# Feature-major products of a fp32 decoder block: the low halves of the weights stored at shifted addresses

## The chip, the cores and the metric

The kernel runs on one core of a Trainium2 chip. The metric is device time of one execution in microseconds: the median of several executions. A profile is taken of one further execution; its span is the time from the first to the last recorded instruction.

The engines are named as in the profile: PE is TensorE (matrix products), PEld its loading of weights, DVE is VectorE, ACT is ScalarE, POOL is GpSimd, SP is SyncE, which here issues the loads of weights from memory.

## The reference

One layer of a decoder trunk on 256 positions of 2048 features in fp32. Cut to what is computed:

```
h = rms_norm(x, norm_mix_pre);  proj = h @ w_in
a_in, b_in, q, kv, nsa_g, merge_g = split(proj)
y_a = conformer_conv(a_in, ...)            # GLU, depthwise conv of 31, LayerNorm, swish, @ w_a_out
y_b = chunked_spatial_gating(b_in, ...)    # gelu, LayerNorm, 128x128 mixing, @ w_b_out
y_c = native_sparse_attention(q, kv, ...)  # compressed, selected and window branches, @ w_c_out
mixed = (g_a * y_a + g_b * y_b + g_c * y_c) @ w_o
x = x + rms_norm(mixed, norm_mix_post)
h = rms_norm(x, norm_ffn_pre)
u = causal_depthwise_conv(h @ w_up);  u_g, u_v = split(u)
x = x + rms_norm((silu(u_g) * u_v) @ w_down, norm_ffn_post)
```

Nearly all of the arithmetic is in the products with `w_in`, `w_up` and `w_down`.

## The kernel before

**Numbers in two parts.** TensorE multiplies in a rounded form of fp32 (float32r, `R` in the code). To keep precision, each operand is split: a head `hi` (the value copied to float32r by ScalarE) and a rest `lo` (the value minus its head, by VectorE). A product is the sum of head x head, head x rest and rest x head.

**Weights.** Each block of weights, 128 partitions x 1024 columns (512 KB), comes by one DMA on SP's queue into one of five `wraw` buffers (`fetch`, line 100). `piece` (line 128) then makes the head with one ScalarE copy (line 143) into one of four `whi` buffers, and the rest with one VectorE subtraction (line 144) into one of four `wlo` buffers. `raw.name` numbers them: `whi72` and `wlo72` belong to `wraw72`. `split2` (line 108) does the same in two halves for the first product of the program.

**Feature-major products.** `ftile` (line 150) computes 128 output features for all 256 positions. Its weights are the stationary operand and come as two pieces (`granule`): k-tiles 0 to 7 and 8 to 15, each k-tile 128 columns, so 512 bytes of a partition's row. The activations are the moving operand: `hT` (first layer) or `h2T` (second layer), laid out as k-tile, part (head, rest), position. `lumps` (line 161) writes the matmuls of one tile in three groups:

- `h(0..7)`: weight heads x both parts of the activation, 512 moving columns (line 172);
- `l(0..15)`: weight rests x the head of the activation, 256 moving columns (line 179);
- `h(8..15)`: as the first, for the last eight k-tiles.

Each matmul has weights of its own, so each has a weight load. The load for the next matmul runs while the present one streams its moving columns. There are 40 such tiles with `hT` (conformer input, gating input, keys and values, queries) and 88 with `h2T` (`w_up`). Of those 88, the first two are written out by hand around the end of the first layer (`up_hi`, `up_lo`, line 1064, with the loop at line 1028 and the `fixed` order at 1078 to 1100), and the third at lines 1125 to 1156. The other products (merge gates, `w_o`, `w_down` and so on) have activations as the stationary operand and weights as the moving one (`mm_t`, `mm`); their weights pass through the same `whi` and `wlo` buffers.

**What sets the order.** Each engine runs its instructions in the order of the built program. The Tile framework sets it from the order of the code, from priorities (`tc.high_priority`) and from explicit chains (`tc.issue_after`). Background work stands in generators (`conv_gen` for the 31-tap convolution, line 475, `sg_gen`, `attn`), from which `pump` takes some after each tile. In the first layer VectorE does the rests, the sums of finished tiles (`fsum`, lines 215 and 217) and that convolution.

**Other names.** `rb2` (line 1118) holds the second layer's scale per position, which `fsum` multiplies in for each of the 88 tiles; `junk` (line 303) is a buffer of 1 KB per partition into which ScalarE writes squares of which only the sum is used.

Of the kernel before, what the change touches and what calls it, by code (L numbers as in the profile page):

```python
# [23 lines left out]
F32 = mybir.dt.float32  # L24
R = mybir.dt.float32r
# [6 lines left out]
T = 256  # L32
KT = 16
# [21 lines left out]
def block(ctx: ExitStack, tc: tile.TileContext, x, xf, fp, cst, rows, sgw, w1, w2, wf_a, wt_bv, wf_bu, wf_c,  # L55
          wt_vs, wf_q, wt_g, wt_p, wt_o, wf_up, wt_dn, wt_dq, out):
    nc = tc.nc
    V, S, PE, G = nc.vector, nc.scalar, nc.tensor, nc.gpsimd

    PZ = ctx.enter_context(tc.tile_pool(name="pz", bufs=1))  # L60
    P0 = ctx.enter_context(tc.tile_pool(name="p0", bufs=1))
# [35 lines left out]
    uid = [0]  # L97
# [7 lines left out]

    fetched = [None]

    def split2(raw):

        hi = P0.tile([128, 1024], R, tag="whi", bufs=4, name="s" + raw.name)  # L110
        lo = P0.tile([128, 1024], R, tag="wlo", bufs=4, name="r" + raw.name)
        for c in (slice(0, 512), slice(512, 1024)):
            with chained():
                a = S.activation(hi[:, c], raw[:, c], AF.Copy)
                v = V.tensor_sub(lo[:, c], raw[:, c], hi[:, c].bitcast(F32))
            chain[:] = [a.ins, v.ins]
        return hi, lo
# [7 lines left out]
            order.enter_context(tc.issue_after(ins))  # L125
        return order

    def piece(src, n, into=None):

        raw = fetch(src, n)  # L130
        if into:
            hl = into.pop(0)
            hi, lo = hl[:, 0], hl[:, 1]
        else:
            hi = P0.tile([128, 1024], R, tag="whi", bufs=4, name=f"whi{uid[0]}")
            lo = P0.tile([128, 1024], R, tag="wlo", bufs=4, name=f"wlo{uid[0]}")
        with ExitStack() as order:
            if behind:
                for ins in behind.pop(0):
                    order.enter_context(tc.issue_after(ins))  # L140
            else:
                order.enter_context(tc.high_priority(offset=int(PR)))
            S.activation(hi[:, :n], raw[:, :n], AF.Copy)  # L143
            V.tensor_sub(lo[:, :n], raw[:, :n], hi[:, :n].bitcast(F32))  # L144
        return hi, lo

    def granule(src):
        return [piece(src[:, a:a + 1024], 1024) for a in (0, 1024)]

    def ftile(src, mov):  # L150

        hs = granule(src)
        ps = PS.tile([128, 2, T], F32, tag="acc", name=f"ps{uid[0]}")
        mm_f(ps, hs, mov)
        return ps
# [5 lines left out]
    def lumps(ps, ws, mov, t=None):  # L161

        ts = slice(0, T) if t is None else slice(t * 128, t * 128 + 128)
        n = 8 * len(ws)
        m = 8 if n > 8 else 7

        def h(ks):
            for k in ks:  # L170
                c = (k % 8) * 128
                ins = PE.matmul(ps[:, :, ts], lhsT=ws[k // 8][0][:, c:c + 128], rhs=mov[:, k, :, ts],  # L172
                                start=(k == 0 and not t), stop=(k == n - 1), skip_group_check=t is not None).ins
            return ins

        def l(ks):
            for k in ks:
                c = (k % 8) * 128
                ins = PE.matmul(ps[:, 1, ts], lhsT=ws[k // 8][1][:, c:c + 128], rhs=mov[:, k, 0, ts], start=False,  # L179
                                stop=False, skip_group_check=True).ins  # L180
            return ins
        return [lambda: h(range(m)), lambda: l(range(n)), lambda: h(range(m, n))]
# [791 lines left out]
    def fixed(eng, op, *args, **kw):  # L974

        with ExitStack() as order:
            order.enter_context(tc.high_priority())
            for ins in seq.get(eng, ()):
                order.enter_context(tc.issue_after(ins))
            seq[eng] = [op(*args, **kw).ins]  # L980
# [45 lines left out]
    for n, (cb, p) in enumerate(HELD):  # L1026
        for i in range(2):
            if n == 0 and i == 0:
                pe_last[0] = mm_o(cb, 1, p, held[n], (i,))
            else:  # L1030
                in_line(mm_o, cb, 1, p, held[n], (i,))
            if (n, i) == (3, 1):
                h2 = P0.tile([128, KT, 2, T], R, tag="hT", name="h2T")
            k = 2 * n + i - 7
            if k == 14:
                order_of(order2)
                fixed(S, S.activation, junk, po[3, 1], AF.Square, accum_out=ss1[1][:, 3:4])
            for k in ([k] if 0 <= k < 14 else [14, 15] if k == 14 else []):
                in_line(enter2, 0, k)
                if k % 4 == 3:  # L1040
                    up = wf_up[k // 8][:, k // 4 % 2 * 1024:k // 4 % 2 * 1024 + 1024]
                    if k < 15:
                        behind.append(tuple(order2))
                        ws2[k // 8].append(piece(up, 1024))
                    else:
                        raw = fetch(up, 1024)
        if p == 7 and cb == 2:
            done_o(cb, 1)
# [12 lines left out]

    def up_lo(f, ks):
        for k in ks:
            ins = PE.matmul(pu2[f][:, 1], lhsT=ws2[f][k // 8][1][:, k % 8 * 128:k % 8 * 128 + 128],
                            rhs=h2[:, k, 0], start=False, stop=False, skip_group_check=True).ins
        return ins

# [7 lines left out]
    fixed(V, V.reduce_sum, v1, ss1[1], axis=AX.X)  # L1075
    fixed(V, V.tensor_scalar, v1, v1, 1.0 / D, EPS, op0=ALU.mult, op1=ALU.add)
    fixed(S, S.activation, r1, v1, AF.Sqrt)
    hi, lo = (P0.tile([128, 1024], R, tag=tag, bufs=4, name=tag + "last") for tag in ("whi", "wlo"))
    fixed(S, S.activation, hi, raw, AF.Copy)
    ws2[1].append((hi, lo))  # L1080
    fixed(V, V.reciprocal, r1, r1)
# [6 lines left out]
    for c in range(4):  # L1088
        if c == 0:
            residual(0)  # L1090
            residual(1)
        for k in quarter[c]:
            in_line(enter2, 1, k)
        if c == 0:
            residual(2)
            fixed(V, V.tensor_mul, y1[:, 1, 1536:], po[3, 1], rw[:, 1536:])
            in_line(up_hi, 1, range(12, KT), 0)
        elif c == 1:
            residual(3)
            fixed(V, V.tensor_sub, lo, raw, hi.bitcast(F32))  # L1100
        if c:
            for f in range(2):
                in_line(up_hi, f, quarter[c - 1], 1)
        for f in range(2):
            in_line(up_lo, f, quarter[c])
# [9 lines left out]
    gl = [P2.tile([128, 11, T], R, tag="gl", bufs=4, name=f"gl{i}") for i in range(4)]  # L1115
    P2b = P2b_ctx.enter_context(tc.tile_pool(name="p2b", bufs=1))
    T1["pool"], T1["bufs"] = P2b, 2
    rb2 = P2b.tile([128, T], F32, name="rb2")

    def small(name, shape=(128, T), dt=F32):  # L1120
        return P2b.tile(list(shape), dt, tag="fa", bufs=5, name=name)

    ones2 = small("ones2", (128, 128))
    G.memset(ones2, 1.0)
    raw = [fetch(wf_up[2][:, a:a + 1024], 1024) for a in (0, 1024)]
    hs = []
    for i in range(2):
        hi, lo = (P0.tile([128, 1024], R, tag=tag, bufs=4, name=f"{tag}f2{i}") for tag in ("whi", "wlo"))
        fixed(S, S.activation, hi, raw[i], AF.Copy)
        fixed(V, V.tensor_sub, lo, raw[i], hi.bitcast(F32))  # L1130
        hs.append((hi, lo))
    with ExitStack() as order:
        order.enter_context(tc.high_priority())
# [109 lines left out]
        return hi, lo  # L1243

    def ring(name):
        return [P0.tile([128, 1024], R, tag=tag, bufs=4, name=f"{tag}{name}") for tag in ("whi", "wlo")]

    class Pair:
        def __init__(self, p):
# [265 lines left out]
```

## Time and profile before

| | us |
|---|---|
| median of 3 executions | 1577.27 |
| lowest, highest | 1576.33, 1577.35 |
| the profiled execution | 1577.51 |
| its span | 1575.8 |

A row of the instruction groups reads: line, engine, operation, output<-inputs, shape, count | busy time in us, mean of one in ns | idle time of the engine just before them in us, and what ended it. A timeline row reads: start and length in us, engine, line, operation, and how many like it follow each other. The length of a merged row runs to the end of its last instruction, and a matmul's own length overlaps the next one's start. In the table by stretches, each engine has its busy time and, in brackets, its instructions.

### The profile page before, as it was taken

Reading aid. Unit: us, or ns where it says so; the run is one execution under the profiler, and the core shown is the slowest. Engines: PE = TensorE matmul, PEld = TensorE weight load, DVE = VectorE, ACT = ScalarE, POOL = GpSimd, SP = SyncE. Lnnn points to the kernel's source line nnn. Section 1 sums busy time; section 2 is a strip of 40 time slices with the busy share of each in tenths; the row PEclk is TensorE's granted clock in tenths of the full one; section 3 lists DMA queues with packets and bytes.
Section 4 is the critical chain, followed back from the end, with each engine's and each line's share of the span. In section 5 each row is a group of like instructions: output and inputs, shape, how many; then the busy total and the mean of one; then the engine's idle time right before and its main releaser. Section 6 shows DMA issues by size and latency. Waiting matters only on the chain.

```text
span 1575.8 us, 22359 instructions
## 1 busy us (share of the span) xinstructions
PE 1564.6 (99%) x8178; PEld 1328.5 (84%) x8178; DVE 1232.3 (78%) x2114; ACT 891.8 (57%) x1442; POOL 19.5 (1%) x50
## 2 busy tenths in 40 slices
PE   9999999999999999999999999999999999999997
PEld 7888889888888787788888888888888888888885
DVE  7899999858866555465557988888777777988997
ACT  7644544447646675644456666565555555555563
POOL 1000020000000000000000000000000000000000
PEclk9999999999999999999999999999999999999999
DMA  9555556665764445556774666666566666666674
GB/s 375 177 196 182 189 176 212 193 197 179 235 200 157 159 137 173 160 187 187 243 250 149 204 191 189 191 189 188 187 188 191 191 191 190 200 203 211 207 235 159
DMA packets 85439, 307.94 MB, mean 195 GB/s; under 512 B 9808, under 2 KB 10832, under 8 KB 84304
## 3 DMA queue, kind: packets, MB, share of 16 engines
q1 hardware_dynamic: 83376, 297.84, 59.2%
q0 software_dynamic: 1520, 8.39, 1.5%
q8 instruction: 64, 1.05, 0.3%
q10 hardware_dynamic: 432, 0.28, 0.1%
q14 instruction: 47, 0.39, 0.1%
HBM read 301.23 MB, written 4.19 MB: 194 GB/s over the span
## 4 chain that ended last, share of the span: by engine, by line
PE 96%; DVE 2%; DMA 1%; issue 0%; ACT 0%; DVEq 0%; POOL 0%; ACTq 0%; POOLq 0%
PE ps L172 29%; PE ps L179 15%; PE pg L193 6%; PE pg L192 6%; PE pg L194 6%; PE pd0b L1264 5%; PE pd1a L1264 4%; PE py L193 3%; PE py L194 3%; PE py L192 3%; PE po L192 2%; PE po L194 2%; PE po L193 2%; PE pd0a L1264 2%; PE pd1b L1264 1%; PE pv L192 1%
## 5 line engine op out<-in xcount | busy, mean ns | idle before, releaser
L144 DVE TENSOR_TENSOR wlo<-wraw,whi 128x1024 fp32r<-128x1024 f32 x440 | 535.9, 1221 | 173.6 <-ACT whi L143 167.0
L143 ACT ACTIVATE whi<-wraw 128x1024 fp32r<-128x1024 f32 x440 | 461.4, 1054 | 244.3 <-PE pg L194 98.0
L172 PE MATMUL ps<-h2T,whi 128*128 128x512 f32 x1360 | 325.0, 391 | 0.0
L172 PEld LDWEIGHTS ps<-h2T,whi 128*128 128x128 f32 x1360 | 249.8, 188 | 48.2
L179 PEld LDWEIGHTS ps<-h2T,wlo 128*128 128x128 f32 x1360 | 174.5, 191 | 6.7
L179 PE MATMUL ps<-h2T,wlo 128*128 128x256 f32 x1360 | 176.6, 283 | 0.0
L172 PE MATMUL ps<-hT,whi 128*128 128x512 f32 x640 | 157.5, 392 | 0.0
L214 ACT ACTIVATE t<-ps 128x256 f32<-128x256 f32 x125 | 47.6, 382 | 185.7 <-PE ps L172 185.3
L194 PE MATMUL pg<-whi,hT 128*128 128x512 f32 x384 | 150.9, 393 | 0.0
L193 PE MATMUL pg<-wlo,hT 128*128 128x512 f32 x384 | 150.7, 392 | 0.0
L192 PE MATMUL pg<-whi,hT 128*128 128x512 f32 x384 | 147.8, 393 | 0.0
L172 PEld LDWEIGHTS ps<-hT,whi 128*128 128x128 f32 x640 | 116.2, 189 | 21.3
L215 DVE TENSOR_TENSOR t<-ps,t 128x256 f32<-128x256 f32 x125 | 52.9, 424 | 68.9 <-ACT t L214 68.2
L475 DVE SCALAR_TENSOR_TENSOR cv<-hb,fps,cv 128x256 f32<-128x256 f32 x240 | 105.7, 484 | 0.8 <-ACT cv L471 0.7
L179 PEld LDWEIGHTS ps<-hT,wlo 128*128 128x128 f32 x640 | 84.8, 190 | 4.6
L179 PE MATMUL ps<-hT,wlo 128*128 128x256 f32 x640 | 87.0, 283 | 0.0
L193 PEld LDWEIGHTS pg<-wlo,hT 128*128 128x128 f32 x384 | 72.1, 188 | 16.2 <-issue 1.1
L194 PEld LDWEIGHTS pg<-whi,hT 128*128 128x128 f32 x384 | 72.1, 188 | 15.1 <-issue 0.7
L192 PEld LDWEIGHTS pg<-whi,hT 128*128 128x128 f32 x384 | 71.8, 188 | 14.7 <-issue 0.3
L980 DVE TENSOR_TENSOR wlowraw<-wraw,whiwraw 128x1024 fp32r<-128x1024 f32 x44 | 53.2, 1223 | 11.8 <-ACT whiwraw L980 10.6
L980 ACT ACTIVATE whiwraw<-wraw 128x1024 fp32r<-128x1024 f32 x44 | 45.7, 1054 | 18.1 <-PE pd0b L1264 14.9
L1194 ACT ACTIVATE fa<-fs,fps 128x256 f32<-128x256 f32 x88 | 52.5, 596 | 1.2 <-DVE fs L217 0.9
(1020 smaller groups left out, 2468.1 us busy)
## 6 DMA issues: line engine op xcount, KB each, us to landing
wraw<-in_wf_up_dram SPq DMA_DIRECT2D x176, 512.0 KB, 4.3
wraw<-in_wt_g_dram SPq DMA_DIRECT2D x96, 512.0 KB, 4.3
wraw<-in_wt_p_dram SPq DMA_DIRECT2D x48, 512.0 KB, 4.2
wraw<-in_wt_dn_dram SPq DMA_DIRECT2D x48, 512.0 KB, 4.4
wraw<-in_wt_dq_dram SPq DMA_DIRECT2D x40, 512.0 KB, 4.7
wraw<-in_wf_a_dram SPq DMA_DIRECT2D x32, 512.0 KB, 4.5
wraw<-in_wt_o_dram SPq DMA_DIRECT2D x32, 512.0 KB, 4.5
wraw<-in_wf_bu_dram SPq DMA_DIRECT2D x16, 512.0 KB, 4.5
```

The costliest lines, as they stand in the source:

```text
L143: S.activation(hi[:, :n], raw[:, :n], AF.Copy)
L144: V.tensor_sub(lo[:, :n], raw[:, :n], hi[:, :n].bitcast(F32))
L172: ins = PE.matmul(ps[:, :, ts], lhsT=ws[k // 8][0][:, c:c + 128], rhs=mov[:, k, :, ts], start=(k == 0 and not t), stop=(k == n - 1), skip_ ...
L179: ins = PE.matmul(ps[:, 1, ts], lhsT=ws[k // 8][1][:, c:c + 128], rhs=mov[:, k, 0, ts], start=False, stop=False, skip_group_check=True).ins
L192: PE.matmul(ps, lhsT=xh, rhs=hi, start=first, stop=False)
L193: PE.matmul(ps, lhsT=xh, rhs=lo, start=False, stop=False)
L194: return PE.matmul(ps, lhsT=xl, rhs=hi, start=False, stop=last).ins
L215: V.tensor_add(t1 if rb is not None else dst, ps[:, 0], t1)
L475: V.scalar_tensor_tensor(ca[:, j], hb[:, j, k:k + T], w(j, k), ca[:, j], op0=ALU.mult, op1=ALU.add)
L980: seq[eng] = [op(*args, **kw).ins]
L1194: S.activation(a, s, AF.Identity, bias=fps[:, C_FB + f:C_FB + f + 1], scale=w[2])
L1264: ins = PE.matmul(bank, lhsT=a[x], rhs=w[y], start=first and j == 0, stop=last and j == 2).ins
```

## The change

Rests of feature-major products get rows of 1152 columns instead of 1024 (`rests`), of which each piece uses 1024 and some left free. `spread(k)` gives the place of k-tile `k` in its row: k-tile 0 at column 0 as before, k-tiles 1 to 14 at 16 columns (64 bytes) past their old place, k-tile 15 at 24 columns (96 bytes) past it. All buffers start at a multiple of 512 bytes, before and after. `apart` writes them: the subtraction of one piece becomes two, k-tile 0 and k-tiles 1 to 7 for the first piece (`first` true), k-tiles 8 to 14 and k-tile 15 for the second. The matmuls read the rests at `spread(k)`; heads, activations and all other products stay where they were. Where rests of other products pass through the same buffers, the first 1024 columns are used as before. The four longer buffers take 2 KB of a partition's memory; `rb2` gives back 1 KB by lying in `junk`.

```diff
+    def rests(name):
+        return P0.tile([128, 1152], R, tag="wlo", bufs=4, name=name)
+
+    def spread(k):
+        return k % 8 * 128 + (0, 16, 24)[(k > 0) + (k == KT - 1)]
...
-            V.tensor_sub(lo[:, :n], raw[:, :n], hi[:, :n].bitcast(F32))
+            if first is None:
+                V.tensor_sub(lo[:, :n], raw[:, :n], hi[:, :n].bitcast(F32))
+            else:
+                apart(lo, raw, hi, first)
...
+    def apart(lo, raw, hi, first, do=None):
+
+        for a, b, to in ((0, 128, 0), (128, 1024, 144)) if first else ((0, 896, 16), (896, 1024, 920)):
+            x = (lo[:, to:to + b - a], raw[:, a:b], hi[:, a:b].bitcast(F32))
+            if do:
+                do(V, V.tensor_sub, *x)
+            else:
+                V.tensor_sub(*x)
+
+    def granule(src, feat=False):
+        return [piece(src[:, a:a + 1024], 1024, first=not a if feat else None) for a in (0, 1024)]
...
-        hs = granule(src)
+        hs = granule(src, True)
...
             for k in ks:
-                c = (k % 8) * 128
+                c = spread(k)
                 ins = PE.matmul(ps[:, 1, ts], lhsT=ws[k // 8][1][:, c:c + 128], rhs=mov[:, k, 0, ts], start=False,
...
-            ins = PE.matmul(pu2[f][:, 1], lhsT=ws2[f][k // 8][1][:, k % 8 * 128:k % 8 * 128 + 128],
+            ins = PE.matmul(pu2[f][:, 1], lhsT=ws2[f][k // 8][1][:, spread(k):spread(k) + 128],
...
-    rb2 = P2b.tile([128, T], F32, name="rb2")
...
+    rb2 = junk.bitcast(F32)
```

In the hand-written part the pieces of the first three `w_up` tiles are split by `apart` in the same way (`fixed` gives them their place in VectorE's order). Line numbers grow by 6 to 18 from the first added lines on: line 144 of before is 151 and 163 in the changed kernel (163 for the split rests), 215 is 233, 217 is 235, 475 is 493.

The order on VectorE, in the second layer. `fa` and `fs` are the tiles of the short convolution after `w_up`, `t1` holds half a tile's sum. Before:

```order
L1196 SCALAR_TENSOR_TENSOR fa27_9452<-fs27_9447,fps_65,fa27_9452 128x254
L144 TENSOR_TENSOR wlo351_9584<-wraw351_9581,whi351_9583 128x1024
L1199 TENSOR_TENSOR fa26_9398<-fa26_9398,fa27_9452 128x256
L1170 TENSOR_TENSOR st6_9572<-fa26_9398 128x128
L1203 TENSOR_TENSOR gl1_7886<-fa26_9398,gh1_7882 128x128
L215 TENSOR_TENSOR t1_348_9506<-ps348_9472,t1_348_9506 128x256
L217 SCALAR_TENSOR_TENSOR fs28_9505<-t1_348_9506,rb2_7892 128x256
L144 TENSOR_TENSOR wlo352_9590<-wraw352_9587,whi352_9589 128x1024
```

After the change:

```order
L163 TENSOR_TENSOR wlo351_9723<-wraw351_9720,whi351_9722 128x128
L163 TENSOR_TENSOR wlo351_9723<-wraw351_9720,whi351_9722 128x896
L1214 SCALAR_TENSOR_TENSOR fa27_9587<-fs27_9582,fps_65,fa27_9587 128x254
L1217 TENSOR_TENSOR fa26_9531<-fa26_9531,fa27_9587 128x256
L1188 TENSOR_TENSOR st6_9711<-fa26_9531 128x128
L233 TENSOR_TENSOR t1_348_9643<-ps348_9609,t1_348_9643 128x256
L235 SCALAR_TENSOR_TENSOR fs28_9642<-t1_348_9643,junk_113 128x256
L163 TENSOR_TENSOR wlo352_9730<-wraw352_9727,whi352_9729 128x896
L163 TENSOR_TENSOR wlo352_9730<-wraw352_9727,whi352_9729 128x128
```

Each rest has become two instructions at the same place; two or three small instructions have changed places with them.

The order on VectorE in the first layer, around the last feature tile of the keys and values (`wlo79` and `wlo80`), where VectorE also works on the gating product (`ub`, `Bt`) and the convolution (`cv`). Before:

```order
L144 TENSOR_TENSOR wlo79_2357<-wraw79_2354,whi79_2356 128x1024
L550 TENSOR_TENSOR ub_1451<-ub_1451,sgf6_2153 128x256
L475 SCALAR_TENSOR_TENSOR cv_118<-hb_116,fps_65,cv_118 128x256 x2
L144 TENSOR_TENSOR wlo80_2363<-wraw80_2360,whi80_2362 128x1024
L475 SCALAR_TENSOR_TENSOR cv_118<-hb_116,fps_65,cv_118 128x256
L550 TENSOR_TENSOR ub_1451<-ub_1451,sgf7_2161 128x256
L475 SCALAR_TENSOR_TENSOR cv_118<-hb_116,fps_65,cv_118 128x256 x2
L217 SCALAR_TENSOR_TENSOR kkv_2187<-t1_74_2233,hb_116 128x256
L215 TENSOR_TENSOR t1_76_2288<-ps76_2255,t1_76_2288 128x256
```

After the change:

```order
L163 TENSOR_TENSOR wlo79_2419<-wraw79_2416,whi79_2418 128x896
L568 TENSOR_TENSOR ub_1483<-ub_1483,sgf4_2142 128x256
L568 TENSOR_TENSOR ub_1483<-ub_1483,sgf5_2150 128x256
L235 SCALAR_TENSOR_TENSOR kcv_1953<-t1_72_2202,hb_116 128x256
L568 TENSOR_TENSOR ub_1483<-ub_1483,sgf6_2209 128x256
L493 SCALAR_TENSOR_TENSOR cv_118<-hb_116,fps_65,cv_118 128x256 x2
L568 TENSOR_TENSOR ub_1483<-ub_1483,sgf7_2217 128x256
L233 TENSOR_TENSOR t1_76_2348<-ps76_2315,t1_76_2348 128x256
L235 SCALAR_TENSOR_TENSOR kkv_2243<-t1_74_2291,hb_116 128x256
L493 SCALAR_TENSOR_TENSOR cv_118<-hb_116,fps_65,cv_118 128x256
L163 TENSOR_TENSOR wlo80_2426<-wraw80_2423,whi80_2425 128x896
L163 TENSOR_TENSOR wlo80_2426<-wraw80_2423,whi80_2425 128x128
```

Here `wlo80` stands behind ten other instructions where it stood behind three, among them the sum of the finished tile `ps76`. Ahead of the next piece, `wlo81`, the program has 128 halves of rests for the 64 whole rests of before, and 155 steps of the convolution for 165.

More of the change, by code (lines that the diff above doesn't have):

```diff
@@ L106, in block @@
     fetched = [None]
+    def rests(name):
+        return P0.tile([128, 1152], R, tag="wlo", bufs=4, name=name)
+    def spread(k):
+        return k % 8 * 128 + (0, 16, 24)[(k > 0) + (k == KT - 1)]
     def split2(raw):
         hi = P0.tile([128, 1024], R, tag="whi", bufs=4, name="s" + raw.name)
-        lo = P0.tile([128, 1024], R, tag="wlo", bufs=4, name="r" + raw.name)
+        lo = rests("r" + raw.name)[:, 0:1024]
         for c in (slice(0, 512), slice(512, 1024)):
@@ L126, in chained, with piece @@
         return order
-    def piece(src, n, into=None):
+    def piece(src, n, into=None, first=None):
         raw = fetch(src, n)
@@ L135, in piece @@
             hi = P0.tile([128, 1024], R, tag="whi", bufs=4, name=f"whi{uid[0]}")
-            lo = P0.tile([128, 1024], R, tag="wlo", bufs=4, name=f"wlo{uid[0]}")
+            lo = rests(f"wlo{uid[0]}")
         with ExitStack() as order:
@@ L143, in piece @@
             S.activation(hi[:, :n], raw[:, :n], AF.Copy)
-            V.tensor_sub(lo[:, :n], raw[:, :n], hi[:, :n].bitcast(F32))
+            if first is None:
+                V.tensor_sub(lo[:, :n], raw[:, :n], hi[:, :n].bitcast(F32))
+            else:
+                apart(lo, raw, hi, first)
         return hi, lo
-    def granule(src):
-        return [piece(src[:, a:a + 1024], 1024) for a in (0, 1024)]
+    def apart(lo, raw, hi, first, do=None):
[7 more added lines that the diff above has]
+        return [piece(src[:, a:a + 1024], 1024, first=not a if feat else None) for a in (0, 1024)]
     def ftile(src, mov):
-        hs = granule(src)
+        hs = granule(src, True)
         ps = PS.tile([128, 2, T], F32, tag="acc", name=f"ps{uid[0]}")
@@ L1043, in block @@
                         behind.append(tuple(order2))
-                        ws2[k // 8].append(piece(up, 1024))
+                        ws2[k // 8].append(piece(up, 1024, first=k % 8 < 4))
                     else:
@@ L1077, in block @@
     fixed(S, S.activation, r1, v1, AF.Sqrt)
-    hi, lo = (P0.tile([128, 1024], R, tag=tag, bufs=4, name=tag + "last") for tag in ("whi", "wlo"))
+    hi, lo = P0.tile([128, 1024], R, tag="whi", bufs=4, name="whilast"), rests("wlolast")
     fixed(S, S.activation, hi, raw, AF.Copy)
@@ L1099, in block @@
             residual(3)
-            fixed(V, V.tensor_sub, lo, raw, hi.bitcast(F32))
+            apart(lo, raw, hi, False, fixed)
         if c:
@@ L1127, in block @@
     for i in range(2):
-        hi, lo = (P0.tile([128, 1024], R, tag=tag, bufs=4, name=f"{tag}f2{i}") for tag in ("whi", "wlo"))
+        hi, lo = P0.tile([128, 1024], R, tag="whi", bufs=4, name=f"whif2{i}"), rests(f"wlof2{i}")
         fixed(S, S.activation, hi, raw[i], AF.Copy)
-        fixed(V, V.tensor_sub, lo, raw[i], hi.bitcast(F32))
+        apart(lo, raw[i], hi, not i, fixed)
         hs.append((hi, lo))
@@ L1245, in ring @@
     def ring(name):
-        return [P0.tile([128, 1024], R, tag=tag, bufs=4, name=f"{tag}{name}") for tag in ("whi", "wlo")]
+        return P0.tile([128, 1024], R, tag="whi", bufs=4, name=f"whi{name}"), rests(f"wlo{name}")[:, 0:1024]
     class Pair:
```

## The prediction

> **What bounds the kernel now.** I read the page from the top first: the span, the busy shares, the slices and the chain.
>
> ```profile
> span 1575.8 us, 22359 instructions
> PE 1564.6 (99%) x8178; PEld 1328.5 (84%) x8178; DVE 1232.3 (78%) x2114; ACT 891.8 (57%) x1442; POOL 19.5 (1%) x50
> ...
> PE   9999999999999999999999999999999999999997
> ...
> PEclk9999999999999999999999999999999999999999
> ...
> PE 96%; DVE 2%; DMA 1%; issue 0%; ACT 0%; DVEq 0%; POOL 0%; ACTq 0%; POOLq 0%
> PE ps L172 29%; PE ps L179 15%; PE pg L193 6%; PE pg L192 6%; PE pg L194 6%; PE pd0b L1264 5%; PE pd1a L1264 4%; PE py L193 3%; PE py L194 3%; PE py L192 3%; PE po L192 2%; PE po L194 2%; PE po L193 2%; PE pd0a L1264 2%; PE pd1b L1264 1%; PE pv L192 1%
> ```
>
> TensorE (PE) is busy in every slice, at the full granted clock, and holds 96% of the chain. What shortens its stream of products shortens the kernel; what another engine does counts only where it makes TensorE wait. The change touches line 179, the product with the rests `wlo`, which is 15% of the chain.
>
> A busy engine need not be a fast one, so I next read the timeline of one product of the second layer, for the step from one matmul to the next.
>
> ```profile
> 901.03 2.08 PE L179 MATMUL ps<-h2T,wlo 128*128 128x256 f32 x16
> 902.94 3.82 PE L172 MATMUL ps<-h2T,whi 128*128 128x512 f32 x16
> 906.60 2.08 PE L179 MATMUL ps<-h2T,wlo 128*128 128x256 f32 x16
> ```
>
> ```profile
> L172 PE MATMUL ps<-h2T,whi 128*128 128x512 f32 x1360 | 325.0, 391 | 0.0
> L179 PE MATMUL ps<-h2T,wlo 128*128 128x256 f32 x1360 | 176.6, 283 | 0.0
> ```
>
> ```profile
> 1009.64 2.89 PE L172 MATMUL ps<-h2T,whi 128*128 128x512 f32 x12
> ```
>
> One feature tile takes 906.60 - 901.03 = 5.57 us, and no wait stands in it. A matmul's own 283 or 391 ns overlaps the next one; the step is found by taking off the last one's time. Rests: (2.08 - 0.283) / 15 = 0.1198 us. Heads, once they run evenly: (2.89 - 0.391) / 11 = 0.2272 us. The 256 further columns of a head cost 107.4 ns, so a step of rests is 107.4 ns of columns and **12.4 ns of something else**. That something is what the change can act on: 128 feature products (40 with `hT`, 88 with `h2T`) x 16 steps x 12.4 ns = 25 us.
>
> Is it the reading of the weights? Two views speak of it. The first step of each run of rests is shorter: from 901.03 to 902.94 are 16 steps in 1.91 us, and 15 of them at 0.1198 leave 0.113 us. And the weight loads of the rests are longer than those of the heads (minimum, median, maximum in ns):
>
> ```profile
> L179 PEld LDWEIGHTS ps<-h2T,wlo x1360: 187/192/192, 866.9 to 1336.9; 128*128 128x128 f32 x195
> ...
> L172 PEld LDWEIGHTS ps<-h2T,whi x1360: 187/188/192, 865.1 to 1338.5; 128*128 128x128 f32 x195
> ```
>
> With a short matmul over it, a load settles at 192 ns; with a long one it keeps 188. So the load and the moving operand do delay each other when both run nearly all the time. In the built program of before, both start at a multiple of 512 bytes in every one of these pairs. The one place with as many moving columns (256) and loads from elsewhere is the compression product, whose `bk` slices lie 32 bytes past a multiple of 512:
>
> ```profile
> 409.32 0.28 PE L616 MATMUL zp<-wlo,bk 128*128 128x256 f32 x1
> ...
> 410.04 0.28 PE L616 MATMUL zp<-wlo,bk 128*128 128x256 f32 x1
> 410.15 0.28 PE L614 MATMUL zp<-whi,bk 128*128 128x256 f32 x1
> ```
>
> Seven steps (six matmuls lie between) take 0.83 us: 0.1186 us each, 1.2 ns less than with both on a multiple. Weak, but in the direction of the change.
>
> **The change, part by part.** *Loads from shifted addresses.* Of 16 loads in a run, 15 move: k-tiles 1 to 14 by 64 bytes and 15 by 96. The load of k-tile 1 lies in the first step, which is already short; 14 steps a run can gain. 14 x 128 = 1792. No row shows a shift of 64 or 96 bytes, so I bound it. Far end: nothing is left but the columns, 12.4 ns each, 22.2 us in all. Next: every step becomes like the first, 119.8 - 113 = 6.8 ns, 12.2 us. Nearest in kind: the 32-byte row, 1.2 ns, 2.2 us. On the losing side: heads that follow a run take (3.82 - 0.391) / 15 = 0.2286 us against 0.2272, 1.4 ns more, which is how much a mismatch between the streams costs in this trace; 1.4 x 1792 = 2.5 us lost. I take the middle of the two nearest rows, a step of 0.1158 us: 4.0 ns x 1792 = **7.2 us gained**, of which 40 x 14 x 4.0 ns = 2.2 us in the first layer and 5.0 us in the second. The long first heads after a run I leave as they are: the change moves no head.
>
> The Trainium skill speaks against this term ("TensorE: Matmul & The Clock Gate", section "Step-by-step: what each phase is for"): TensorE has two independent read ports, and loading the next tile's weights takes no read bandwidth from the running matmul. By that rule no address matters and the sum would have no gain; the trace's 192 against 188 ns does not fit it well, but no run here shows the ports themselves.
>
> *Split rests on VectorE.* Each of 256 rests becomes one subtraction of 128 columns and one of 896: 256 more instructions. The group of the whole rest and one of 128 columns, and how they stand back to back:
>
> ```profile
> L144 DVE TENSOR_TENSOR wlo<-wraw,whi 128x1024 fp32r<-128x1024 f32 x434 | 529.8, 1224 | 173.6 <-ACT whi L143 167.0 <-issue 0.4
> ```
>
> ```profile
> 1012.11 1.23 DVE L144 TENSOR_TENSOR wlo<-wraw,whi 128x1024 fp32r<-128x1024 f32 x1
> 1013.26 0.29 DVE L1170 TENSOR_TENSOR gl<-st,gh 128x128 fp32r<-128x128 f32 x1
> 1013.46 0.48 DVE L1195 SCALAR_TENSOR_TENSOR fa<-fs,fps,fa 128x255 f32<-128x255 f32 x1
> ```
>
> The next instruction starts 1.15 us after a whole rest and 0.20 us after 128 columns: 1.06 ns a column and 0.065 us for each instruction. So a split costs 0.065 us, 256 x 0.065 = 16.6 us of VectorE in all; by full durations (1.22 against 0.29 + 1.09) it would be 0.15 us each. Whether TensorE sees any of it depends on the stage:
>
> ```profile
> core 0: us, PE busy (x) PEld busy (x) DVE busy (x) ACT busy (x) POOL busy (x), PEclk, DMA share, GB/s
> 100.00:200.00 100.00, 100.00 (x577) 88.18 (x576) 97.98 (x186) 48.25 (x68) 0.00 (x0) 1.00 0.57 187
> ...
> 225.00:250.00 25.00, 25.00 (x176) 24.07 (x175) 25.00 (x50) 11.99 (x21) 0.84 (x2) 1.00 0.70 214
> ...
> 900.00:1000.00 100.00, 100.00 (x577) 88.39 (x576) 86.21 (x157) 59.46 (x101) 0.00 (x0) 1.00 0.63 190
> ```
>
> In the second layer VectorE is 86% busy or less; two splits, 0.13 us in 5.57, leave it below 90%, and TensorE's own products hide them: cost nothing. In the first layer VectorE is full, because the convolution's steps (line 475) fill it. There the program's order is the cover: ahead of the rests of `wraw81` it has 64 splits more (64 x 0.065 = 4.2 us), and 155 steps of the convolution where there were 165 (ten at 0.40 us, by a pair in the next rows, = 4.0 us less). These ten come later, where TensorE waits for none of them. What is left is the room between the rests and their product:
>
> ```profile
> 226.81 1.23 DVE L144 TENSOR_TENSOR wlo<-wraw,whi 128x1024 fp32r<-128x1024 f32 x1
> ...
> 228.67 0.89 DVE L475 SCALAR_TENSOR_TENSOR cv<-hb,fps,cv 128x256 f32<-128x256 f32 x2
> ```
>
> ```profile
> 229.76 2.08 PE L179 MATMUL ps<-hT,wlo 128*128 128x256 f32 x16
> ```
>
> The rests end at 228.04 and are wanted at the ninth of these matmuls, 229.76 + 8 x 0.12 = 230.7: **2.7 us of room**, the narrowest kind of place in that stage. TensorE comes there 32 x 14 x 4.0 ns = 1.8 us earlier, and just these rests (`wlo80`) now stand behind another product's sum (the order above), about 1 to 3 us later. The wait lies between nothing and 2.1 us; I take 1.0 us, nearer the middle since later pieces have the convolution's slack again.
>
> *The rest.* The rows of the rests grow by 512 bytes in each of 4 buffers, and `rb2` moves into `junk`: no instruction more. `junk` is written by ScalarE alone before `rb2` and again in the down projection, long after the last reader. No DMA is added and SP's queue keeps its order. On TensorE only the first layer's order changes (which product's heads stand between another's rests); the count of products stays, so I cost it at nothing, with 16 x 1.4 = 22 ns for each switch from rests to heads more or fewer.
>
> **Sum**, against the profiled execution's 1577.5 us (span 1575.8 and 1.7 around it; the median of the runs shown is 1577.27): 1577.5 - 7.2 + 1.0 = **1571.3 us**.
>
> **The rivals.** *The address does not matter.* For it: heads of 512 columns carry the same 12 ns (0.2272 us for 214.8 ns of columns), so it may be a fixed price of a matmul. Against it: the first step and the 32-byte row are shorter. Time: 1577.5 + 0 to 1.0, **1578**. This is also the case in which the change does not do what it says. It is the outcome that the Trainium skill's section named above would give.
>
> *Only what 32 bytes showed:* 1577.5 - 2.2 + 0.5 = **1575.8**.
>
> *The shift frees the read altogether.* The steps fall below the first step's 0.113 us towards 0.1074: 12.2 to 22.2 us, less about 2 us of VectorE in the first layer, where the whole gain cannot be kept: **1558 to 1567**. For it: a delay of 12 ns that vanishes once both streams keep apart; against it, no step of that kind in the trace.
>
> *VectorE becomes the bound of the first layer.* If a split costs its full duration, 0.15 us, and the ten delayed steps give no cover (because the rests wait for ScalarE and not behind the convolution), 64 x 0.15 = 9.6 us stand against 2.7 us of room: TensorE waits 6.9 us between 60 and 250 us. With the second layer's gain at the 32-byte value (1.5 us) that is 1577.5 + 6.9 - 1.5 = **1583**. It decides once a split costs over (2.7 + 1.5 + 3.2) / 64 = 0.116 us there. Against it: the trace's 0.065 and the full cover in the order.
>
> **Numbers.** Forecast 0.47 (1566 to 1575); read freed altogether 0.16; only the 32-byte gain 0.12; address without effect 0.16; VectorE the bound, or a shift that clashes more, 0.09. About 0.2% (3.2 us) is what a measurement of this kernel can tell from no change: faster means below 1574.1, slower above 1580.4. Faster: nearly all of the forecast (0.44), the freed read 0.16 and a part of the 32-byte case 0.03, 0.63. Slower: 0.09 and a little of the no-effect case, 0.11. Same: 0.26. The range leaves out the upper half of the last rival and the extreme of the freed read: 1561 to 1580.
>
> **What would show it.** The step of rests from the timeline, (length of a run of 16 less 0.283) / 15: 0.116 forecast, 0.120 without effect, under 0.113 freed. The median load of line 179's group falls from 192 to 188 or less. A feature tile's period of 5.57 us falls to 5.51. VectorE's rests show groups of 128 and 896 columns, and the pair's step 0.065 us over the whole one's. In the window from 200 to 250 us a wait of TensorE for `wlo` of some 1 us in all. Wrong would be: periods unchanged in the second layer; waits on `wlo` there; or a longer step of the heads, which would mean that the delay has only moved.

## The result, and the profile after

| | us |
|---|---|
| before, median of 4 runs | 1577.22 (1576.33 to 1577.35) |
| changed, median of 4 runs | 1563.93 (1563.13 to 1564.66) |
| ratio | 0.9917, 95% interval 0.9900 to 0.9934 |
| profiled execution, before and after | 1577.51 and 1564.14 |

The change makes the kernel 13.3 us faster, 0.8%. The forecast was 1571.3 with a range from 1561 to 1580. The direction was right, and it is the places of the rests that make the gain, but the gain is a little over twice the one forecast.

The page of the changed kernel (span; busy time of each engine; the chain that ended last, by engine):

```profile
span 1562.4 us, 22642 instructions
...
PE 1550.5 (99%) x8178; PEld 1316.9 (84%) x8178; DVE 1244.9 (80%) x2370; ACT 889.8 (57%) x1442; POOL 20.2 (1%) x50
...
PE 96%; DVE 2%; DMA 1%; issue 0%; ACT 0%; DVEq 0%; ACTq 0%
```

The picture is as before: TensorE busy throughout and 96% of the chain. VectorE has 256 instructions more and 12.6 us more busy time. So the gain must lie in the pace of TensorE. The timeline of a tile of the second layer in the changed kernel (line 197 is line 179 of before, 190 is 172):

```profile
896.21 1.99 PE L197 MATMUL ps<-h2T,wlo 128*128 128x256 f32 x16
898.04 3.80 PE L190 MATMUL ps<-h2T,whi 128*128 128x512 f32 x16
901.67 1.99 PE L197 MATMUL ps<-h2T,wlo 128*128 128x256 f32 x16
```

The period is 901.67 - 896.21 = 5.46 us instead of 5.57. The run of rests is shorter by 0.09, and the 16 heads by 0.02. The starts of all matmuls in both traces give the account. By a step is meant the time from one matmul's start to the next one's.

| TensorE, sum of steps | after less before, us |
|---|---|
| line 179 (rests), 2016 matmuls | -10.4 |
| line 172 (heads), 2016 matmuls | -2.2 |
| warm-up matmuls at the start | -0.3 |
| all other lines together | -0.4 |

The mean step of all rests, the hand-written tiles among them, fell from 119.7 to 114.6 ns, that of the heads from 228.8 to 227.7 ns. Position by position in runs of 16, the steps of rests were 113.4, 119.2 and then 120.0 ns. Now they are 113.2 to 113.5 for the first fourteen, then 117.3 and 119.2. The heads behind a run were 233.4, 235.7, 228.4, 232.4 and 230.8 ns before they settled at 226.7. Now they are 232.8, 231.0, 226.8 and so on. The weight loads of the rests have come down with them (minimum, median, maximum in ns):

```profile
L197 PEld LDWEIGHTS ps<-h2T,wlo x1360: 187/188/192, 862.7 to 1323.7; 128*128 128x128 f32 x195
```

Their median is 188 ns, where it was 192.

One pair of figures the prediction did not have: a settled step is now 113.3 ns with 256 moving columns and 226.7 ns with 512, twice as much.

On VectorE the groups by shape show the split, and the list of who waited for whom shows what TensorE waited for in the whole execution:

```profile
L163 DVE TENSOR_TENSOR wlo<-wraw,whi 128x896 fp32r<-128x896 f32 x253 | 274.7, 1086 | 8.4 <-ACT whi L149 4.0
L151 DVE TENSOR_TENSOR wlo<-wraw,whi 128x1024 fp32r<-128x1024 f32 x181 | 220.5, 1223 | 156.3 <-ACT whi L149 155.5
...
L163 DVE TENSOR_TENSOR wlo<-wraw,whi 128x128 fp32r<-128x128 f32 x253 | 71.3, 284 | 3.7 <-ACT whi L149 3.3
```

```profile
engine line waited for: us in total, times, longest us
PE warm L302 <- POOL wz L299: 1.4, 1, 1.4
PE pv L416 <- ACT swraw L120: 0.7, 1, 0.7
PE pd1a L1282 <- DVE wlowraw L998: 0.6, 1, 0.6
```

None of the three waits is for a rest of a feature tile. Yet VectorE is full in the first layer, and busier than before in the second:

```profile
core 0: us, PE busy (x) PEld busy (x) DVE busy (x) ACT busy (x) POOL busy (x), PEclk, DMA share, GB/s
...
100.00:200.00 100.00, 100.00 (x592) 88.46 (x591) 99.99 (x222) 49.75 (x70) 0.00 (x0) 1.00 0.58 188
900.00:1000.00 100.00, 100.00 (x586) 88.27 (x585) 90.27 (x200) 61.85 (x105) 0.00 (x0) 1.00 0.61 193
```

In 100 us of the second layer TensorE now starts 586 matmuls, where it started 577.

### The profile page after: what moved, and what is told of

Same layout as the page of the kernel before. It is cut to its first block, busy times and chain, and to the rows that moved or that the text cites. A ratio compares the mean times of both kernels' runs of the same rounds, so it can differ in the third digit from the quotient of the medians.

```text
span 1562.4 us, 22642 instructions
## 1 busy us (share of the span) xinstructions
PE 1550.5 (99%) x8178; PEld 1316.9 (84%) x8178; DVE 1244.9 (80%) x2370; ACT 889.8 (57%) x1442; POOL 20.2 (1%) x50
## 4 chain that ended last, share of the span: by engine, by line
PE 96%; DVE 2%; DMA 1%; issue 0%; ACT 0%; DVEq 0%; ACTq 0%
PE ps L190 29%; PE ps L197 15%; PE pg L211 6%; PE pg L210 6%; PE pg L212 6%; PE pd0b L1282 5%; PE pd1a L1282 4%; PE py L211 3%; PE py L212 3%; PE py L210 3%; PE po L210 2%; PE po L211 2%; PE po L212 2%; PE pd0a L1282 2%; PE pd1b L1282 1%; PE pv L210 1%
## 5 line engine op out<-in xcount | busy, mean ns | idle before, releaser
L151 DVE TENSOR_TENSOR wlo<-wraw,whi 128x1024 fp32r<-128x1024 f32 (+1 forms) x187 | 226.4, 1215 | 156.3 <-ACT whi L149 155.5
L163 DVE TENSOR_TENSOR wlo<-wraw,whi 128x896 fp32r<-128x896 f32 (+1 forms) x506 | 325.7, 685 | 12.1 <-ACT whi L149 7.3
L197 PEld LDWEIGHTS ps<-h2T,wlo 128*128 128x128 f32 x1360 | 166.9, 188 | 6.7
L197 PE MATMUL ps<-h2T,wlo 128*128 128x256 f32 x1360 | 168.9, 277 | 0.0
L190 PEld LDWEIGHTS ps<-hT,whi 128*128 128x128 f32 x640 | 115.8, 188 | 20.9
```

Source lines behind the costliest of these rows:

```text
L163: V.tensor_sub(*x)
```

## The experiments

The theory at the start: rests and moving operand delay each other when both start on a multiple of 512 bytes; the split on VectorE is hidden. Its rivals: the split or the moved order makes the gain, or the split costs something that the shift has to pay for.

### The split alone, and a uniform shift

The first kernel keeps the split and puts every rest back.

```diff
-        return k % 8 * 128 + (0, 16, 24)[(k > 0) + (k == KT - 1)]
+        return k % 8 * 128
-        for a, b, to in ((0, 128, 0), (128, 1024, 144)) if first else ((0, 896, 16), (896, 1024, 920)):
+        for a, b, to in ((0, 128, 0), (128, 1024, 128)) if first else ((0, 896, 0), (896, 1024, 896)):
```

> The change with its split subtractions but every rest back at its old place (multiples of 512 bytes). Theory (the address makes the gain, the split is hidden): step of rests 0.120 us as before, no waits of TensorE for rests, time 1577 +- 1.5. Rival A (the split and the moved order on VectorE cost something that the shift pays for): 1578.5 to 1580, with waits between 200 and 250 us. Rival B (the gain comes from the split or the order, not the address): 1564 and a step of 0.113.

Measured: 1576.04 us against 1576.56 for the kernel before beside it, ratio 0.9996 (0.9987 to 1.0005). The rests of its timeline are those of before, 16 in 2.08 us:

```profile
895.22 2.08 PE L197 MATMUL ps<-h2T,wlo 128*128 128x256 f32 x16
897.13 3.82 PE L190 MATMUL ps<-h2T,whi 128*128 128x512 f32 x16
```

So the split costs nothing that can be measured, and it gains nothing: the addresses make the whole gain. This kernel has the same instructions as the changed one, in the same order on TensorE, VectorE and ScalarE. Only addresses differ, and with them the time (1576.0 against 1563.9). The Trainium skill says in "TensorE: Matmul & The Clock Gate", section "Step-by-step: what each phase is for", that loading the next tile's weights takes no read bandwidth from the running matmul. To conclude from it that addresses don't matter would be wrong here: the place of those weights sets the pace. Through what the addresses act no run shows.

The second kernel shifts all sixteen k-tiles by 64 bytes, with one subtraction a piece.

```diff
+        return k % 8 * 128 + 16
+        for a, b, to in ((0, 1024, 16),):
```

> All 16 k-tiles 64 bytes past, so one subtraction per piece and no split. Theory (address): steps of rests 0.113 as in the changed kernel; k-tile 0 and 15 at 64 change only the first and last step and the heads behind a run; time 1564 +- 2. Rival A (split costs on VectorE): 1562 to 1563. Rival B (the special places of k-tiles 0 and 15 carry the shorter heads, 2.2 us in the changed kernel): 1566.

Measured: 1572.61 us, ratio 0.9973 (0.9963 to 0.9984), 4 us of the 13. All three expectations missed it. Its timeline and its loads:

```profile
899.37 2.05 PE L197 MATMUL ps<-h2T,wlo 128*128 128x256 f32 x16
901.26 3.82 PE L190 MATMUL ps<-h2T,whi 128*128 128x512 f32 x16
```

```profile
L197 PEld LDWEIGHTS ps<-h2T,wlo x1360: 187/188/193, 865.5 to 1333.1; 128*128 128x128 f32 x195
```

A run takes 2.05 us, neither 2.08 nor 1.99. By position, steps 0 to 14 lie between 117.3 and 118.5 ns, from the very first, and the heads behind are those of before. So k-tile 0, which the changed kernel leaves where it was, is no detail: in these runs of 16, leaving it in place is worth some 4 ns in *every* later step. The load's median of 188 ns is the same as in the changed kernel, so it isn't the sign to look at. The theory that a shift as such removes the clash fell here.

The same trace has something else. In the first layer the 16 rests of many tiles come as two runs of eight, with heads between them:

```profile
119.59 1.11 PE L197 MATMUL ps<-hT,wlo 128*128 128x256 f32 x8
120.53 0.86 PE L190 MATMUL ps<-hT,whi 128*128 128x512 f32 x3
121.23 1.07 PE L197 MATMUL ps<-hT,wlo 128*128 128x256 f32 x8
122.14 3.13 PE L190 MATMUL ps<-hT,whi 128*128 128x512 f32 x13
125.11 1.11 PE L197 MATMUL ps<-hT,wlo 128*128 128x256 f32 x8
```

All loads of rests here are 64 bytes past their old place. Yet the run behind three heads is short (1.07 us) and the others are not. Over the whole trace, all twelve runs of eight that stand behind one, two, three or five heads end in steps of 113 or 114 ns, some of them after up to four longer ones. All 33 that stand behind four, six, seven or more heads have steps of 117 to 119 ns throughout. In the kernel before, no such run settles below 117. So the short pace needs the shift, but whether a shifted run takes it depends also on what ran just ahead of it.

### Curves of the shift

One kernel gives each tile another uniform shift, eleven in turn (no split; `lo = lo[:, shift:shift + 1024]`).

> Each feature tile has its rests at another shift: 0, 16, 32, 48, 64, 80, 96, 128, 192, 256 and 512 bytes in turn, the same for all its k-tiles. Theory (two streams that start on the same place clash): 0 and 512 give 0.120 us a step, 64 gives 0.113, 32 about 0.1186 as the compression rows had, and the larger ones 0.113. Rival (only the multiple of 64 or an odd multiple of it counts): 128 and 256 give 0.120 again. Time about 1567.

It took 1576.0 us in one execution. Five runs of its timeline, shifted by 0, 64, 96, 128 and 256 bytes in this order:

```profile
889.07 2.08 PE L208 MATMUL ps<-h2T,wlo 128*128 128x256 f32 x16
...
911.33 2.05 PE L208 MATMUL ps<-h2T,wlo 128*128 128x256 f32 x16
...
922.47 2.04 PE L208 MATMUL ps<-h2T,wlo 128*128 128x256 f32 x16
928.00 2.08 PE L208 MATMUL ps<-h2T,wlo 128*128 128x256 f32 x16
...
939.14 2.08 PE L208 MATMUL ps<-h2T,wlo 128*128 128x256 f32 x16
```

Means of 8 to 10 tiles each, from the starts in the trace:

| shift, bytes | 0 | 16 | 32 | 48 | 64 | 80 | 96 | 128 | 192 | 256 | 512 |
|---|---|---|---|---|---|---|---|---|---|---|---|
| first step, ns | 113.3 | 113.5 | 117.8 | 119.1 | 118.2 | 115.9 | 118.4 | 124.2 | 117.7 | 113.4 | 113.9 |
| steps 2 to 15, ns | 119.9 | 118.6 | 118.4 | 118.3 | 117.7 | 118.7 | 117.3 | 120.2 | 117.8 | 119.9 | 120.0 |
| eight heads behind, ns | 1841 | 1856 | 1856 | 1841 | 1841 | 1866 | 1841 | 1823 | 1867 | 1841 | 1841 |

Two things are read from it. A shift of 256 or 512 bytes acts like none, as if the pattern repeated after 256 bytes (other pairs 256 bytes apart were not run). And in these runs of 16, no uniform shift brings the steps behind the first near 113.4 ns. The 32-byte row agrees with the compression product of before (118.6 ns), on which a part of the forecast rested.

The next kernel does the same to the heads and leaves the rests.

> The kernel before with the heads of the feature tiles shifted in the same way and the rests left on multiples of 512: does the 12 ns over the columns in a step of heads (0.2272 us) come from the same clash? Theory (same clash): at 64 bytes the heads' step falls to 0.220 or so, 2016 x 6.8 x share of shifted tiles, time about 1566 with all shifts, and the rests stay at 0.120. Rival (a fixed price, or a load that is over long before a long matmul ends): 0.2267 at every shift, time 1577.

It took 1580.9 us, slower. The mean step of heads was 228.5 ns at 0 (228.7 at 512), and between 229.2 and 233.8 at every other shift (233.0 at 64). No uniform shift makes a head's step shorter. That fits the pair of figures above: a settled head, with 226.7 ns, already goes at the pace to which the changed kernel brings the rests.

### What keeps a run short

What distinguishes the changed kernel from the uniform shift is its start. The new theory: a run keeps the state in which it starts, and the jump between k-tiles 0 and 1 holds it. Eleven patterns by turns, written with as many subtractions as a pattern needs:

```diff
+    PATS = [[0] + [64] * 14 + [96], [0] + [64] * 15, [0, 64] + [256] * 14, [0, 0] + [64] * 14, [64] + [128] * 15,
+            [64] + [256] * 15, [0] + [32] * 15, [0] + [128] * 15, [0] + [192] * 15, [0] + [96] * 15, [0] + [16] * 15]
```

> What earlier runs showed: with all 16 rests of a tile 64 bytes past, a step is 0.1177 us, with k-tile 0 left in place 0.1134. Here eleven patterns of shifts take turns by tile: the changed kernel's; 0 then 64; 0, 64, then 256; 0, 0, then 64; 64 then 128; 64 then 256; and 0 then 32, 128, 192, 96 or 16 for the rest. Theory (the run keeps the state in which it starts: a first load in step with the heads gives the short first step, and a jump before the second step keeps it): 0 then 64, 128 or 192 give 0.1134; 0, 0, then 64 gives 0.118; patterns that start at 64 give 0.118. Rival (only k-tiles 1 to 14 at 64 count, k-tile 0 matters for its own step alone): 0, 0, then 64 gives 0.1134 from the third step on. 256 counts as 0 in both (it did in the curve): 0, 64, then 256 tells if the state holds without the shift.

The timeline of its rests in the second layer; the tiles come in the order of the patterns, from the first:

```profile
888.13 1.99 PE L219 MATMUL ps<-h2T,wlo 128*128 128x256 f32 x16
893.59 1.98 PE L219 MATMUL ps<-h2T,wlo 128*128 128x256 f32 x16
899.06 2.07 PE L219 MATMUL ps<-h2T,wlo 128*128 128x256 f32 x16
904.62 2.05 PE L219 MATMUL ps<-h2T,wlo 128*128 128x256 f32 x16
910.15 2.07 PE L219 MATMUL ps<-h2T,wlo 128*128 128x256 f32 x16
915.70 2.08 PE L219 MATMUL ps<-h2T,wlo 128*128 128x256 f32 x16
921.31 2.06 PE L219 MATMUL ps<-h2T,wlo 128*128 128x256 f32 x16
926.88 2.05 PE L219 MATMUL ps<-h2T,wlo 128*128 128x256 f32 x16
932.42 1.98 PE L219 MATMUL ps<-h2T,wlo 128*128 128x256 f32 x16
937.88 2.04 PE L219 MATMUL ps<-h2T,wlo 128*128 128x256 f32 x16
943.41 2.06 PE L219 MATMUL ps<-h2T,wlo 128*128 128x256 f32 x16
```

Three rows are short: the changed kernel's pattern, 0 then 64, and 0 then 192. Means of 8 to 12 tiles:

| pattern | first three steps, ns | mean of 16, ns | eight heads behind, ns |
|---|---|---|---|
| 0, 64 ..., 96 | 113.3, 113.2, 113.4 | 114.0 | 1823 |
| 0, 64 ... | 113.4, 113.3, 113.3 | 113.3 | 1840 |
| 0, 192 ... | 113.2, 113.3, 113.4 | 113.3 | 1840 |
| 0, 64, 256 ... | 113.3, 113.4, 119.1 | 119.1 | 1841 |
| 0, 0, 64 ... | 113.3, 119.1, 117.6 | 117.6 | 1838 |
| 64, 128 ... | 118.4, 112.4, 116.8 | 119.1 | 1836 |
| 64, 256 ... | 117.4, 120.9, 120.0 | 119.8 | 1867 |
| 0, then 32, 128, 96, 16 | 113.3 to 117.4 first | 118.3, 117.9, 117.1, 118.3 | 1840 to 1856 |

For runs of 16 behind settled heads (heads that have come down to 226.7 ns) the theory held where it mattered most. With the jump one k-tile late (0, 0, 64) the run has already lost the short step and does not get it back: 117.6. With the jump in time and then a return to a multiple of 256, the short step is lost in the very next one. So **both are needed there**: a first load in place, and 64 bytes (or 192) from the second load on. It was wrong for 128, which it had put with 64 and 192.

It isn't the whole rule. The runs of eight above came to 113 ns with no load in place, and without a jump. The changed kernel's own runs of seven or eight agree: those that start behind k-tile 0, and so at 64 bytes, come to the short pace behind one, two, three or five heads (eight of eight), and have steps of 117 to 121 ns behind four, six, seven or eight (ten of ten). That is part of why its rests average 115.2 ns in the first layer and 114.0 in the second.

### The moving operand

The same distances can be made by moving `hT` and `h2T` 64 bytes along instead, in the kernel before.

```diff
-    hT = P0.tile([128, KT, 2, T], R, tag="hT", name="hT")
+    hT = P0.tile([128, 8320], R, tag="hT", name="hT")[:, 16:8208].rearrange("p (k a t) -> p k a t", k=KT, a=2)
```

> The kernel before with the moving operand (hT and h2T) 64 bytes past a multiple of 512 and all weights on it. Theory (the distance between the two starts counts, not the load's own address): rests about 0.118 us a step as with a uniform shift, heads longer than 0.2287 on average as when the heads' loads were shifted (0.231 to 0.234); time 1577 to 1590. Rival (the load's own address counts): 0.120 and 0.2287, time 1577.

It took 1577.6 us, but not because nothing happened. The rests have a mean step of 115.5 ns in runs of 16 (7.5 us less in all). The products at lines 192 to 194 are 7.0 us longer, and the heads average 229.4 ns. Neither expectation had this mean, shorter than any uniform shift of the loads gave in such runs. It hides two kinds of run: in the second layer, whole runs take turns with steps of 113.3 and of 117.8 ns, all 85 of them, at the same distances (1.98 and 2.04 us in the timeline below).

The last kernel puts both 64 bytes along, the changed kernel's rests and the moving operand (with one buffer less in a small ring, to make room).

> The changed kernel with the moving operand (hT, h2T) 64 bytes past as well, so that k-tiles 1 to 14 of the rests and their moving operand start at the same place again (one small buffer ring has 4 instead of 5 buffers, to make room). With the moving operand alone at 64 the rests' step was 0.1155 on average and the rest of the program 6.4 us longer. Theory (the distance between the two starts counts): distance 0 again, the step settles at 0.120 as before; time above 1577 by the longer rest. Rival (the loads' own jump from k-tile 0 to 1 keeps the short state): 0.1134.

It took 1584.6 us. Timelines of the two kernels, first the moving operand alone:

```profile
900.11 1.98 PE L179 MATMUL ps<-h2T,wlo 128*128 128x256 f32 x16
901.92 3.82 PE L172 MATMUL ps<-h2T,whi 128*128 128x512 f32 x16
905.58 2.04 PE L179 MATMUL ps<-h2T,wlo 128*128 128x256 f32 x16
```

and both:

```profile
902.09 2.07 PE L197 MATMUL ps<-h2T,wlo 128*128 128x256 f32 x16
904.00 2.22 PE L190 MATMUL ps<-h2T,whi 128*128 128x512 f32 x9
```

With both on the same offset the rests are back at a mean of 119.7 ns a step, as before the change, though not step for step: the runs take turns with means of 119.2 and 119.9 ns. The jump between loads does not help by itself; what counts is the place of the load against that of the moving operand. That it is the distance *alone* is not shown. The slow half of the runs with the moving operand at 64 (117.8) is where uniform loads at 64 and 192 were; what lets the other half run at 113.3 is not shown; in the trace the two kinds simply follow each other.

### The last k-tile, and the heads

What do the 96 bytes of k-tile 15 do? The changed kernel with 64 there:

```diff
+        return k % 8 * 128 + (0, 16)[k > 0]
+        for a, b, to in ((0, 128, 0), (128, 1024, 144)) if first else ((0, 1024, 16),):
```

> The changed kernel with k-tile 15 at 64 bytes like 1 to 14, so one split fewer a tile. Theory (96 bytes buys shorter heads behind the run at a longer last two steps): steps 0.1134 to the end, heads behind a run back at 1841 ns for eight instead of 1826; 15 ns x 128 = 1.9 us lost, 2 x about 4 ns x 128 = 1 us won: 1564.5 to 1566. Rival (96 does nothing): 1563.5. Rival (a split costs on VectorE): below 1563.

Measured 1564.71 us, ratio 0.9923 (0.9910 to 0.9937), beside 0.9917 for the changed kernel: not to be told apart by time. In its trace the 16 rests take 1813 ns instead of 1824, and the eight heads behind 1841 instead of 1824, as expected; the net 6 ns a tile are 0.8 us. It also has 128 splits fewer and is no faster, which speaks once more against a cost of the split.

A kernel with eleven tails looked for a better end.

> Eleven tails by turns after (0, then 64 up to k-tile 13): the last two k-tiles at (64,64), (64,96), (64,128), (64,160), (64,192), (64,80), (64,112), (64,256), (64,288), (96,96), (128,128). Measured so far for 16 rests plus the eight heads behind: (64,64) 3653 ns, (64,96) 3646. Theory (the heads behind a run are set by the distance that the last loads leave, and a tail pays for them in its last steps): heads between 1823 and 1858, with (64,128) at 1826 as the uniform 128 had; no tail gains more than 10 ns over 96. Rival (the heads' 13 ns are free to be won): some tail has 113.4 to the end and heads at 1826, 3640 or less.

It took 1564.5 us. Rests plus eight heads came to 3653 ns for (64,64), 3647 for (64,96), 3653 for (64,128) and (64,192), 3660 to 3682 for the others, and 3640 for (64,80), with heads of 1819: the least. So the theory's limit of 10 ns held, but not its claim on (64,128), whose heads are 1834. The tail (64,80) was then run as a kernel of its own, beside the changed one.

> The changed kernel with k-tile 15 at 80 bytes instead of 96. From the tails: 3640 ns for 16 rests and eight heads against 3647, so 7 ns x 126 tiles = 0.9 us less than the changed kernel beside it: about 1563. Rival (the tail's gain is lost elsewhere or too small to see): the same time as the changed kernel within 0.5 us.

> The changed kernel once more, unchanged, on the same chip as the run before it: 1563.9 +- 0.8, ratio to before 0.992.

Measured: 1563.46 us with 80 bytes (ratio 0.9915, 0.9901 to 0.9928), 1563.70 with 96 (0.9916, 0.9903 to 0.9930). The two can't be told apart. The changed kernel repeats its gain.

The heads, last, with patterns that start in place, in the kernel before:

```diff
+    PATS = [[0]*16, [0]+[64]*15, [0]+[192]*15, [0]*9+[64]*7, [0]*9+[192]*7, [0]*8+[64]*8, [0]*8+[192]*8,
+            [0]+[64]*7+[0]*8, [0]*9+[32]*7, [0]*9+[96]*7, [0]*9+[128]*7]
```

> The kernel before with the heads of feature tiles shifted by patterns that start in place (0 then 64, 0 then 192, k-tiles 8 to 15 alone, and so on), rests left in place: does the heads' step of 0.2267 us fall as the rests' step does when the first load stays? Theory (a state that a short matmul alone can keep; a head's load is over long before its matmul): 0.2267 or longer at every pattern, time 1577 to 1581. Rival (the same state): 0.220 for the patterns 0 then 64 and 0 then 192, time 1573 to 1575.

It took 1582.1 us, and the heads' mean step rose from 228.8 to 231.1 ns; by pattern it lies between 229.9 and 233.2. (A run of 16 heads ends with eight of the next tile, so each pattern also meets its neighbour.) What shortens 256 moving columns does not shorten 512.

## Why the prediction was right in direction and short in size

**What bounds the kernel.** Right: TensorE's pace, with no wait that mattered, before and after. The steps of rests were the right place to look, and the first, shorter step was the right sign: it is the pace that the changed kernel keeps.

**The 12.4 ns "of something else".** This reading did not hold. It took the difference between a step of heads and one of rests, 107.4 ns, as the price of 256 columns, which supposes that both carry the same extra time. In the changed kernel the same difference is 226.7 - 113.3 = 113.4 ns, as much as a whole step of rests, and nothing is left over. By these figures a settled step of rests was 6.7 ns too long (120.0 against 113.3), not 12.4, and the far end of the range, 22.2 us, could not have been reached.

**The gain of the shift: the term that was mis-sized.** The prediction put it at 4.0 ns on each of 1792 steps, 7.2 us, as "the middle of the two nearest rows", 113 and 118.6 ns. The rests gained 10.4 us: 113.3 to 113.5 ns in steps 2 to 14 of a run, near its "next" bound of 12.2 us, and less in the last two steps. The mistake was to read the two rows as points on one scale, on which a greater distance clashes less. The curve shows no such scale: in runs of 16, uniform shifts from 16 to 192 bytes all have mean steps between 117.3 and 120.2 ns, in no order of distance. The compression product (32 bytes) belongs with these. The first step of a run has the other pace, 113.3, and the one mean found near the forecast's 115.8 (115.5, with the moving operand shifted) is a mixture of runs at 113.3 and at 117.8. Which pace a run takes depends on how it begins, and on what runs ahead of it. The prediction passed over this: it noted that k-tile 0 keeps its place and drew nothing from it.

By layers, the rests gained 2.8 us in the first (forecast 2.2) and 7.6 in the second (forecast 5.0).

**The heads behind a run: a term set to nothing.** "I leave [them] as they are: the change moves no head." They gained 2.2 us. The run with k-tile 15 at 64 bytes shows that the 96 bytes do it, by 17 ns a tile in the heads at the cost of 11 ns in the last two rests.

**VectorE.** Set at 1.0 us in the first layer; the split alone cost nothing, and no wait for a rest of a feature tile is in the trace, though VectorE is busy for 99.99 of 100 us there. That the program's order covers the split was right; the room at `wlo80` did not run out. The price on VectorE itself was right too: from start to start, the two halves of a rest take 1.205 us where the whole one took 1.142, 0.063 us more.

**The sum.** 10.4 + 2.2 and 0.7 us from small differences elsewhere, the warm-up among them, give the 13.3 us. The measured 1563.9 lies inside the whole range but below the band of the forecast itself (1566 to 1575). That the total still came within the range owes something to the bounds set for a rival.

**The rivals.** That the address has no effect: refuted by the split alone. Only the 32-byte gain: that is about what the uniform shift reached (4 us). The read freed altogether, 1558 to 1567: the time fell into its bounds, but its mechanism did not show, since no step of rests in the changed kernel is below 113 ns. VectorE as the bound: refuted, as was its price of 0.15 us a split.

## What to carry to other kernels

Where TensorE is busy all the time, look at the steps between matmuls position by position, not at their mean: one position that is shorter than its equals shows a pace that the others could have. Where weights are loaded under short matmuls, the places of the two operands are worth a few kernels with many patterns taking turns, but a pattern found for 256 moving columns is not one for 512, and one k-tile, or a few matmuls ahead of it, can decide a whole run. When two rows differ, ask whether they are points on a scale or two states before taking a middle, and look behind a mean for the kinds of run in it.

## What the runs showed of the hardware that was not expected

- The steps of rests have a memory. In runs of 16 behind settled heads, the same load at 64 bytes gives 113.3 ns behind a first load at 0 and 117.7 behind a first load at 64; once lost (0, 0, 64), the short step did not come back in the 14 steps that followed.
- The same addresses can have two paces. With every rest at 64 bytes, runs of eight behind one, two, three or five heads came to 113 ns (12 of 12), and those behind four, six or more stayed at 117 to 119 (33 of 33). With the moving operand at 64 bytes, whole runs of 16 took turns at 113.3 and 117.8 ns.
- A settled step was 113.3 ns with 256 moving columns and 226.7 with 512, twice as much, once the rests went at the short pace.
- Shifts of 256 and 512 bytes act like none (119.9 and 120.0 against 119.9 ns).
- After a run of short matmuls, five longer ones pay up to 9 ns each (235.7 against 226.7) before they settle, and where the last load lies changes how many of them do.
- With `hT` 64 bytes along as the stationary operand, the 1332 matmuls of 512 columns at lines 192 to 194 that load it became 7.4 us longer, 5.6 ns each.

Why a run takes one pace or the other is not settled by these runs: they show which addresses, and which order of matmuls, lead to which, and not what inside the engine or the memory holds them.
